# The second norm of a hybrid block: scaled rows and plain transposes in two parts, and a pool whose tiles move by 128 bytes

## The chip, the cores and the metric

The kernel runs on one core of one Trainium2 chip. The metric is the device time of one execution in microseconds, given as the median of several runs. TensorE is called PE (its weight loads PEld), VectorE DVE, ScalarE ACT, GpSimd POOL and SyncE SP; SP's queue issues nearly all transfers of the part that is changed.

## The reference

The block computes one layer on 1024 tokens of width 1024, in float32:

```python
u = modulate(rms_norm(h, ln1_g), shift1, scale1)
mix = token_mixer(u, ...)                  # attention and a recurrent mix, gated, then @ w_o
h = h + gate1[:, None, :] * mix
u2 = modulate(rms_norm(h, ln2_g), shift2, scale2)
h = h + gate2[:, None, :] * conv_ffn(u2, w_up, conv_w, conv_b, w_down)
return rms_norm(h, final_g)

def rms_norm(x, gain):
    return x * rsqrt(mean(x * x, axis=-1) + 1e-6) * gain

def modulate(xn, shift, scale):
    return xn * (1 + scale[:, None, :]) + shift[:, None, :]
```

`conv_ffn` multiplies `u2` (1024x1024) with `w_up` (1024x5632), applies a convolution of width 3 along the tokens, SiLU and a gate, and multiplies with `w_down` (2816x1024). The change concerns the third and fourth line: how `u2` comes out of `h`.

## The kernel before, in words

**Numbers.** A float32 matrix product is made of three products in a faster format (`F32R`): each operand is split into a high and a low part (`split`: ACT casts the high part, DVE subtracts it), and the parts are multiplied high by high, low by high and high by low (`PARTS`). A product of two plain float32 operands (`mm` with F32 tiles) is the other form.

**Stages.** The first norm and the projections, attention and the recurrent mix, the gated branches (`br_part`), then the part that matters here: the output projection with `w_o` (`wo_mm`, `wo_row`), the second norm with its turn (`norm2`, `turn2`), the feed-forward's first product for 22 column tiles of 128 (`up_product`), its second product (`dn_mm`) and the last norm.

**The output projection.** The tokens are eight row tiles of 128, `t` = 0 to 7. For a row tile 48 products of 128x512 (8 `kt`, two column halves `c`, three parts) fill two PSUM banks. The stationary operands are the merged rows, high and low (`mg_hl`; the low part of rows 0 to 3 is `mgl` in pool `se`), the moving ones `wo_hi` and `wo_lo`. Row tiles 0 to 2 are interleaved, and between them stand 16 products of one column with the modulation vectors (`mod_2`, `mod_part_steps`). `wo_row` then takes the row tile: per column half, DVE multiplies PSUM by the gate and adds the result to `h_sb[t]`, and ACT squares it and leaves the row sums in a column of `ssq`. The temporary `x` comes from `row_tmp` for `t` below 5, and from the tag `xq` behind it. SP stores the row to `d_h[t]`, from where the last stage reads it.

**The second norm and the turn.** `norm2(half)` adds the two column halves of the row sums of four row tiles, makes the factors with two ACT instructions (`rms_rstd`) and, on DVE, four diagonal matrices of 128x128 in the tile `dg`: the identity times the factor of each row. `turn2(half, kt, ...)` then makes one bank of `u2` turned: four float32 products of a 128x128 block of `h_sb` (stationary) with that row tile's diagonal matrix (moving), which turns the block and scales its columns by the factors at once. ACT takes the bank out with the modulation's scale and shift (`A2`, `m2`), by row of the turned block. A half needs 8 banks, or 32 products.

**Order.** PE's instructions run in the order written. The first half's turns stand between row tile 4's and row tile 5's products. Each bank is split into the feed-forward's operands `B11` (pool tiles `b`) and `B21` (tiles `f`). Behind that point the order of SP, DVE, ACT and POOL is the written one too; ahead of it a scheduler puts the instructions of those four in order. Behind row tile 7's products, `norm2(1)` runs on DVE and ACT while PE makes the feed-forward's first two products (`X` and `W` of column tile 0); the second half's turns follow in two groups of 16 products, with column tile 1's product `X` between them and `W` behind them.

**The feed-forward's first product** uses Strassen's scheme in Winograd's form: seven products per column tile in place of eight. Its moving operands are sums of the halves of `u2`, each split into high and low: `T3`, `T2`, `T4`, `T1`, `B22`, `B11` and `B21`. DVE and ACT make `T3`, `T2`, `T4`, `T1` and `B22` behind the second half's turns, while PE runs the first products of column tiles 0 and 1 (`T_split`). The low parts of `T1` lie in `e1` and `e5`, the high parts of `B22` in `e2` and `e3`; in the profile they are `T_e` and `B_e`, and the parts of the same operands in the pool `sm` are `T_m` and `B_m`. The stationary operands are sums of pieces of `w_up`, split too (`up_make`), from two loads per column tile (`up_load`); those of tile 1 are loaded into the slots that `h_sb[0]` and `h_sb[1]` had. All 12 products of one of the seven share a bank, and the profile shows them as `X`, `Y` or `W` by its name. DVE's subtractions and ACT's casts for the next stationary operands run a few products ahead (`up_ahead`).

**Pools.** The pool `se` (variable `hp`) holds the tags `e0` to `e5`, `xq` (five buffers), `s` (two), `dg` (one) and the tile `ssq2` of 128 bytes per partition. A tile's place follows from the order in which tags are first used; `ssq2` was the last.

Of the kernel before, what the change touches and what calls it, by code (L numbers as in the profile page):

```python
# [9 lines left out]
F32 = mybir.dt.float32  # L10
F32R = mybir.dt.float32r
AF = mybir.ActivationFunctionType
ALU = mybir.AluOpType
# [4 lines left out]
KT = 8  # L18
NH = 512
# [113 lines left out]
def hybrid_block(ctx: ExitStack, tc: tile.TileContext, a, out):  # L133
    nc = tc.nc
# [3 lines left out]
    def mm(o, lhsT, rhs, start, stop, more=False):  # L138

        weave.mm_cost(o, lhsT, rhs)  # L140
        nc.tensor.matmul(o, lhsT, rhs, start=start, stop=stop, skip_group_check=more)  # L141

    def transpose(o, i, eye):
        weave.now += 0.84 * max(math.prod(i.shape[1:]), i.shape[0])
        nc.tensor.transpose(o, i, eye)
# [4 lines left out]
    tt, stt, ts = nc.vector.tensor_tensor, nc.vector.scalar_tensor_tensor, nc.vector.tensor_scalar  # L150
# [24 lines left out]
    ident, ones = f32(eye_r), f32(C("ones"))  # L175
# [33 lines left out]
    m2 = cp.tile([128, 16], F32, name="m2")  # L209
    A2 = cp.tile([128, 8], F32, name="A2")  # L210
# [135 lines left out]
    with ExitStack() as es:  # L346
# [66 lines left out]
        with tc.tile_pool(name="st", bufs=1) as st, tc.tile_pool(name="stp", bufs=2, space=PS) as stp, \  # L413
                tc.manual_schedule(engines={mybir.EngineType.SP, mybir.EngineType.DVE, mybir.EngineType.Activation}):
            ssq = st.tile([128, 8], F32, name="ssq")
# [765 lines left out]
    def bank(k, name):  # L1181
        return pb.tile([128, NH], F32, tag="big", name=name) if k > 5 else pz.tile([128, NH], F32, tag=f"p{k}", name=name)
# [47 lines left out]
    ww_st.close()  # L1230
    pools["m"] = ctx.enter_context(tc.tile_pool(name="sm", bufs=1, side="right", reuse_waits="tile"))
    pools["e"] = hp = ctx.enter_context(tc.tile_pool(name="se", bufs=1, side="right", reuse_waits="tile"))

    def pairs(tags, name, dt=F32R):

        ts_ = [slot(tag, f"{name}_{tag}", dt) for tag in tags]
        return [ts_[k // 2][:, k % 2 * NH : k % 2 * NH + NH] for k in range(2 * len(tags))]
# [6 lines left out]
    def split(hi, lo, src):  # L1244
        nc.scalar.copy(hi, src)  # L1245
        tt(lo, src, f32(hi), op=ALU.subtract)  # L1246
# [3 lines left out]
    wo = {}  # L1250
# [56 lines left out]
    for x in range(2):  # L1307
        for n in range(8):
            if x or n:
                k = 8 * x + n + 1  # L1310
# [26 lines left out]

    d_h = dr.tile([8, 128, D], F32, name="d_h")
    d_g = dr.tile([7, 128, NP, NH], F32, name="d_g")
    ssq = hp.tile([128, 32], F32, name="ssq2")  # L1340
    def norm2(half):

        dg = hp.tile([128, NH], F32, tag="dg", name=f"dg{half}", bufs=1).rearrange("p (j s) -> p j s", s=128)
        hs = slice(half * 4, half * 4 + 4)
        rs = slice(8 + half * 4, 12 + half * 4)
        tt(ssq[:, rs], ssq[:, rs], ssq[:, hs], op=ALU.add)
        rms_rstd(ssq[:, rs], ssq[:, rs])
        for j in range(4):
            ts(dg[:, j, :], ident, ssq[:, rs][:, j : j + 1], None, op0=ALU.mult)
        return dg  # L1350

    def turn2(half, kt, dg, k, dst):

        ps = bank(k, f"tr{half}_{kt}")
        for j in range(4):
            mm(ps[:, j * 128 : j * 128 + 128], h_sb[half * 4 + j][:, kt * 128 : kt * 128 + 128], dg[:, j, :], start=True, stop=True)
        nc.scalar.activation(dst, ps, AF.Identity, scale=A2[:, kt : kt + 1], bias=m2[:, kt : kt + 1])


    PARTS = ((0, 0), (1, 0), (0, 1))  # L1360
# [13 lines left out]
    def wo_row(t, ps):  # L1374

        for c in range(2):
            cs = slice(c * NH, c * NH + NH)
            x, h = row_tmp[2 * t + c] if t < 5 else hp.tile([128, NH], F32, tag="xq", name=f"wo{t}_{c}", bufs=5), h_sb[t][:, cs]
            tt(x, ps[c], g1b[:, cs], op=ALU.mult)
            tt(h, h, x, op=ALU.add)  # L1380
            nc.scalar.activation(x, h, AF.Square, accum_out=ssq[:, 8 * c + t : 8 * c + t + 1])
        nc.sync.dma_start(d_h[t], h_sb[t])
# [3 lines left out]
    def T_tiles(key, tags):  # L1386
        T[key] = halves(tags, key)
# [243 lines left out]
    for t in range(4, 8):  # L1631
        h_load(t)
    up_load(0)
    dg = norm2(0)
    ps = wo_do(4, 0)
    wo_row(4, ps)

    T_tiles("B11", [f"b{k}" for k in range(4)])
    T_tiles("B21", [f"f{k}" for k in range(4)])
    uf = pairs(("e2", "e3", "e1", "e5"), "uf", F32)  # L1640
    for kt in range(KT):
        turn2(0, kt, dg, 4 + kt % 4, uf[kt])
        split(*(T["B11" if kt < 4 else "B21"][x][kt % 4] for x in range(2)), uf[kt])
    up_load(1)
    ctx.enter_context(tc.manual_schedule(engines={mybir.EngineType.SP, mybir.EngineType.DVE, mybir.EngineType.Activation,
                                                  mybir.EngineType.Pool}))
    for t, k in ((5, 2), (6, 6), (7, 4)):
# [4 lines left out]
            for f in up_ahead(2 * (t - 4)):  # L1652
                f()
        wo_row(t, ps)
    dg = norm2(1)


    early = pairs(("a7",), "Ze", F32)
    steps = up_to(len(plan))
    t1, b21 = uf[0:4], uf[4:]  # L1660
    U = [pairs(tags, f"u2{j}", F32) for j, tags in enumerate((("m8", "m9"), ("m10", "m11")))]
    T_tiles("T3", [f"h{k}" for k in range(4)])

    def T_split(key, srcs, sums=()):
# [10 lines left out]
    for n in range(4):  # L1675
        up_evac(*next(steps))
        if n == 1:
            for f in up_ahead(8):
                f()
        if n in (1, 2):  # L1680
            kts = (0, 1) if n == 1 else (2, 3)
            for kt in kts:
                for j in range(2):
                    turn2(1, kt + 4 * j, dg, 2 + kt % 2 * 2 + j, U[j][kt])
            for kt in kts:
                tt(t1[kt], U[0][kt], t1[kt], op=ALU.subtract)
                tt(U[0][kt], U[1][kt], U[0][kt], op=ALU.subtract)
                nc.scalar.copy(T["T3"][0][kt], U[0][kt])
                if kt % 2:
                    for x in kts:  # L1690
                        tt(T["T3"][1][x], U[0][x], f32(T["T3"][0][x]), op=ALU.subtract)
# [291 lines left out]
```

## Time and profile before

| what | value |
|---|---|
| median of 3 runs | 1682.1 us |
| runs | 1679.19, 1686.33, 1682.1 us |
| profiled execution, first to last instruction (span) | 1679.9 us |
| PE busy | 1630.3 us (97% of the span) |
| DVE busy | 1219.1 us (73%) |
| ACT busy | 806.3 us (48%) |
| granted TensorE clock, mean | 0.993 |
| second norm's turns, first half | 993.57 to 1000.63 us |
| second norm's turns, second half | 1038.90 to 1042.38 and 1045.25 to 1048.73 us |

The page gives the profiled execution no time beside its span. The span lies 2.2 us under the median of the runs and inside their range.

How to read the rows: a time is in microseconds from the span's start. In a timeline a row has start, length, engine, line, operation, out<-in, shape and count; instructions of one kind are merged, and the length runs from the first one's start to the last one's end. In brackets stands how long the engine had been idle before and what ended that. Matmuls are pipelined, so that a single one's length is more than its distance to the next: distances are taken from starts. In the list by line a row ends with the busy time, the mean length in ns and the idle time ahead of it. In the chain a row has start, length, engine, output and line. Line 141 is the helper `mm` and line 145 the helper `transpose`, so PE's rows are told apart by tile names, in which buffer numbers are left out.

### The profile page before, as it was taken

The numbers are of one execution on the slowest core, as the hardware profiler recorded it, in microseconds if no ns is written. First come the engines' busy times: TensorE is split into PE (matmuls) and PEld (weight loads), VectorE is DVE, ScalarE is ACT, GpSimd is POOL, SyncE is SP. The second block draws the span as 40 slices with busy tenths as digits, with TensorE's granted clock in tenths as the row PEclk, the third lists the DMA queues.
The fourth block names the chain that finished last, engine by engine and source line by source line (L and its number), as shares of the span: only waits on it lengthen the run. The fifth ranks groups of instructions, "written<-read, shape, count | busy, mean of one in ns | idle before, by whom it ended". The sixth has DMA issues, their size and how long they took to land.

```text
span 1679.9 us, 26265 instructions
## 1 busy us (share of the span) xinstructions
PE 1630.3 (97%) x9870; PEld 1344.6 (80%) x9870; DVE 1219.1 (73%) x2402; ACT 806.3 (48%) x1481; POOL 131.2 (8%) x151
## 2 busy tenths in 40 slices
PE   7999999999999999999999999999999999999998
PEld 7777777787877778888878888888888888888886
DVE  5786787878866635888778455897777777786677
ACT  5563334434445446676633243654444444455455
POOL 0011001111111011212022000000000000000000
PEclk9999999999999999999999999999999999999999
DMA  8487644443332228434197420133322323584463
GB/s 332 143 322 233 181 124 123 130 120 98 100 112 88 89 67 202 126 108 128 35 335 262 177 88 38 63 120 111 109 95 94 119 95 107 182 276 152 130 211 108
DMA packets 121503, 240.79 MB, mean 143 GB/s; under 512 B 40032, under 2 KB 48608, under 8 KB 121376
## 3 DMA queue, kind: packets, MB, share of 16 engines
q1 hardware_dynamic: 112896, 220.74, 40.2%
q0 software_dynamic: 8480, 18.37, 4.3%
q8 instruction: 78, 1.28, 0.3%
q14 instruction: 49, 0.40, 0.1%
HBM read 173.51 MB, written 65.54 MB: 142 GB/s over the span
## 4 chain that ended last, share of the span: by engine, by line
PE 74%; DVE 14%; DMA 5%; ACT 3%; issue 2%; SPq 1%; DVEq 0%; ACTq 0%
PE X L141 13%; PE D L141 12%; PE Y L141 6%; PE wo L141 5%; PE ps_rkv L141 5%; PE br L141 5%; PE gt L141 4%; PE W L141 3%; PE rk_ps L141 3%; PE qk L141 2%; PE lg L141 2%; PE ov L141 2%; DVE E L780 2%; DVE t L778 2%; PE tr L141 2%
## 5 line engine op out<-in xcount | busy, mean ns | idle before, releaser
L141 PE MATMUL D<-op,op 128*128 128x512 f32 x924 | 209.8, 389 | 0.0
L141 PEld LDWEIGHTS D<-op,op 128*128 128x128 f32 x924 | 173.3, 188 | 36.3 <-DVE op L1246 0.3
L141 PE MATMUL X<-T_m,S 128*128 128x512 f32 x440 | 107.2, 390 | 0.2 <-ACT x L1522 0.2
L141 PEld LDWEIGHTS X<-T_m,S 128*128 128x128 f32 x440 | 82.4, 188 | 18.3 <-ACT x L1522 0.6
L1245 ACT CAST op<-g 128x512 fp32r<-128x512 f32 x77 | 47.8, 621 | 73.7 <-PE D L141 48.5
L1246 DVE TENSOR_TENSOR op<-g,op 128x512 fp32r<-128x512 f32 x77 | 53.0, 688 | 41.4 <-ACT op L1245 41.1
L1482 DVE SCALAR_TENSOR_TENSOR c<-ab,vec,c 128x512 f32<-128x512 f32 x88 | 65.9, 749 | 19.5 <-ACT c L1485 17.9
L778 DVE TENSOR_TENSOR t<-E,M 128x60 f32<-128x60 f32 (+24 forms) x248 | 57.6, 232 | 25.7 <-DMA M<-sm 20.3
L1446 DVE TENSOR_TENSOR S<-ur,S 128x512 fp32r<-128x512 f32 x66 | 45.5, 691 | 35.9 <-ACT S L1442 35.8
L1442 ACT CAST S<-ur 128x512 fp32r<-128x512 f32 x66 | 41.0, 622 | 55.8 <-DVE ur L1435 30.6
L1446 DVE TENSOR_TENSOR A<-ur,A 128x512 fp32r<-128x512 f32 x64 | 44.0, 688 | 30.9 <-ACT A L1442 30.7
L274 DVE TENSOR_TENSOR lo_in<-raw_in,hi_in 128x512 fp32r<-128x512 f32 x84 | 56.5, 712 | 12.5 <-PE gt L141 4.6
L141 PE MATMUL Y<-T_h,A 128*128 128x512 f32 x264 | 63.4, 389 | 0.0
L141 PE MATMUL Y<-T_h,S 128*128 128x512 f32 x264 | 63.3, 389 | 0.0
L272 ACT CAST hi_in<-raw_in 128x1024 fp32r<-128x1024 f32 x42 | 43.8, 1047 | 40.1 <-PE ps_rkv L141 23.2
L1048 ACT ACTIVATE P<-lg,nm 128x896 f32<-128x896 f32 (+3 forms) x64 | 47.5, 743 | 29.0 <-DVE nm L1044 20.8
L141 PE MATMUL X<-B_b,A 128*128 128x512 f32 x252 | 60.8, 390 | 0.0
L141 PE MATMUL W<-B_f,A 128*128 128x512 f32 x252 | 60.6, 389 | 0.0
L780 DVE TENSOR_TENSOR E<-E,t 128x60 f32<-128x60 f32 (+24 forms) x248 | 54.9, 221 | 5.7
L141 PEld LDWEIGHTS Y<-T_h,A 128*128 128x128 f32 x264 | 49.5, 188 | 10.4
L141 PEld LDWEIGHTS Y<-T_h,S 128*128 128x128 f32 x264 | 49.5, 188 | 10.3
L1442 ACT CAST A<-ur 128x512 fp32r<-128x512 f32 x64 | 39.9, 623 | 34.1 <-PE X L141 29.4
(475 smaller groups left out, 4130.9 us busy)
## 6 DMA issues: line engine op xcount, KB each, us to landing
raw_in<-in_w_in SPq DMA_DIRECT2D x50, 512.0 KB, 3.9
wm<-in_w_mod SPq DMA_DIRECT2D x48, 512.0 KB, 7.2
ur<-in_w_up SPq DMA_DIRECT2D x44, 512.0 KB, 4.2
g<-d_g SPq DMA_DIRECT2D x35, 512.0 KB, 4.1
d_g<-gs SPq DMA_DIRECT2D x44, 256.0 KB, 2.0
d_g<-c SPq DMA_DIRECT2D x33, 256.0 KB, 4.4
d_st<-qh SPq DMA_DIRECT2D x64, 128.0 KB, 2.4
stA<-d_st POOLq DMA_DIRECT2D x8, 1024.0 KB, 6.4
```

Of the source, the lines that this page charges most:

```text
L141: nc.tensor.matmul(o, lhsT, rhs, start=start, stop=stop, skip_group_check=more)
L272: nc.scalar.copy(hi, raw)
L274: nc.vector.tensor_tensor(lo[:, c : c + NH], raw[:, c : c + NH], f32(hi[:, c : c + NH]), op=ALU.subtract)
L778: tt(tv, E32[:, 0:J, s : s + 1].to_broadcast([128, J, W]), M32[:, s : s + 1, s + 1 : 32].to_broadcast([128, J, W]), op=ALU.mult)
L780: tt(E32[:, 0:J, s + 1 : 32], E32[:, 0:J, s + 1 : 32], tv, op=ALU.add)
L1048: nc.scalar.activation(e[:, 0:n], lg[:, 0:n], AF.Exp, bias=nm[:, 0:1], accum_out=nm[:, 1:2])
L1245: nc.scalar.copy(hi, src)
L1246: tt(lo, src, f32(hi), op=ALU.subtract)
L1442: nc.scalar.copy(hi, src)
L1446: tt(lo, src, f32(hi), op=ALU.subtract)
L1482: stt(c, ab[:, x + hf * NH : x + hf * NH + NH], V("conv_w", 22 * x + i), c, op0=ALU.mult, op1=ALU.add)
```

## The change

- `norm2(t0, t1)` adds the sums and makes the factors of row tiles `t0` to `t1 - 1`, and no diagonal matrices. It is called for 0 to 3, for 4 to 6 and for 7.
- `scale_row(t)` multiplies a row tile by its factor: tiles 0 to 6 in place, on DVE, over 1024 columns; tile 7 into the slot `m11`, half on DVE and half on ACT.
- `turn2` takes several banks at a time and fills them with transposes against the identity. In the first half ACT and DVE take the banks out in turn (`split_evac`); in the second ACT alone, as before. In the second half's first group row tile 7's blocks come last, behind those of the other three.
- The first half is turned in two parts of four banks: `kt` 0 to 3 where all eight were, and 4 to 7 behind row tile 5's product, into banks 4, 5, 0 and 1.
- For row tiles 5 to 7 `wo_row` takes its first temporary from the tag `dg`, which is free now, and its second from `xq`.
- `ssq2` is the first tile of the pool `se`. The other tiles of that pool start 128 bytes further on than before, and which of the five `xq` buffers a tile gets changes with the row temporaries.

```diff
     pools["e"] = hp = ctx.enter_context(tc.tile_pool(name="se", bufs=1, side="right", reuse_waits="tile"))
+    ssq = hp.tile([128, 32], F32, name="ssq2")
...
-    ssq = hp.tile([128, 32], F32, name="ssq2")
-    def norm2(half):
-
-        dg = hp.tile([128, NH], F32, tag="dg", name=f"dg{half}", bufs=1).rearrange("p (j s) -> p j s", s=128)
-        hs = slice(half * 4, half * 4 + 4)
-        rs = slice(8 + half * 4, 12 + half * 4)
+    def norm2(t0, t1):
+
+        hs, rs = slice(t0, t1), slice(8 + t0, 8 + t1)
         tt(ssq[:, rs], ssq[:, rs], ssq[:, hs], op=ALU.add)
         rms_rstd(ssq[:, rs], ssq[:, rs])
-        for j in range(4):
-            ts(dg[:, j, :], ident, ssq[:, rs][:, j : j + 1], None, op0=ALU.mult)
-        return dg
-
-    def turn2(half, kt, dg, k, dst):
-
-        ps = bank(k, f"tr{half}_{kt}")
-        for j in range(4):
-            mm(ps[:, j * 128 : j * 128 + 128], h_sb[half * 4 + j][:, kt * 128 : kt * 128 + 128], dg[:, j, :], start=True, stop=True)
-        nc.scalar.activation(dst, ps, AF.Identity, scale=A2[:, kt : kt + 1], bias=m2[:, kt : kt + 1])
+
+    normed = {}
+
+    def scale_row(t, dst=None):
+        r = ssq[:, 8 + t : 9 + t]
+        if dst is None:
+            ts(h_sb[t], h_sb[t], r, None, op0=ALU.mult)
+            dst = [h_sb[t][:, c * NH : c * NH + NH] for c in range(2)]
+        else:
+            ts(dst[0], h_sb[t][:, 0:NH], r, None, op0=ALU.mult)
+            nc.scalar.activation(dst[1], h_sb[t][:, NH:], AF.Copy, scale=r)
+        normed[t] = dst
+
+    def turn2(half, kts, ks, dsts, rows=((0, 1, 2, 3),), split_evac=False):
+
+        pss = [bank(k, f"tr{half}_{kt}") for kt, k in zip(kts, ks)]
+        for js in rows:
+            for kt, ps in zip(kts, pss):
+                for j in js:
+                    c0 = kt % 4 * 128
+                    transpose(ps[:, j * 128 : j * 128 + 128], normed[half * 4 + j][kt // 4][:, c0 : c0 + 128], ident)
+        for n, (kt, ps, dst) in enumerate(zip(kts, pss, dsts)):
+            A, B = A2[:, kt : kt + 1], m2[:, kt : kt + 1]
+            if split_evac and n % 2:
+                ts(dst, ps, A, B, op0=ALU.mult, op1=ALU.add)
+            else:
+                nc.scalar.activation(dst, ps, AF.Identity, scale=A, bias=B)
...
-            x, h = row_tmp[2 * t + c] if t < 5 else hp.tile([128, NH], F32, tag="xq", name=f"wo{t}_{c}", bufs=5), h_sb[t][:, cs]
+            x, h = row_tmp[2 * t + c] if t < 5 else hp.tile([128, NH], F32, tag=("dg", "xq")[c], name=f"wo{t}_{c}", bufs=(1, 5)[c]), h_sb[t][:, cs]
...
-    dg = norm2(0)
+    norm2(0, 4)
+    for t in range(4):
+        scale_row(t)
     ps = wo_do(4, 0)
     wo_row(4, ps)
...
-    for kt in range(KT):
-        turn2(0, kt, dg, 4 + kt % 4, uf[kt])
-        split(*(T["B11" if kt < 4 else "B21"][x][kt % 4] for x in range(2)), uf[kt])
+
+    def turn_first(kts, ks):
+        turn2(0, kts, ks, [uf[kt] for kt in kts], split_evac=True)
+        for kt in kts:
+            split(*(T["B11" if kt < 4 else "B21"][x][kt % 4] for x in range(2)), uf[kt])
+
+    turn_first(range(4), (4, 5, 6, 7))
     up_load(1)
...
         wo_row(t, ps)
-    dg = norm2(1)
+        if t == 5:
+            turn_first(range(4, 8), (4, 5, 0, 1))
+        elif t == 6:
+            norm2(4, 7)
+            for r in (4, 5, 6):
+                scale_row(r)
...
     U = [pairs(tags, f"u2{j}", F32) for j, tags in enumerate((("m8", "m9"), ("m10", "m11")))]
+    norm2(7, 8)
+    scale_row(7, U[1][2:])
...
             kts = (0, 1) if n == 1 else (2, 3)
-            for kt in kts:
-                for j in range(2):
-                    turn2(1, kt + 4 * j, dg, 2 + kt % 2 * 2 + j, U[j][kt])
+            turn2(1, [kt + 4 * j for kt in kts for j in range(2)], (2, 3, 4, 5), [U[j][kt] for kt in kts for j in range(2)],
+                  rows=((0, 1, 2), (3,)) if n == 1 else ((0, 1, 2, 3),))
```

## The prediction

> **What bounds the kernel now.** I read the page first, then the busy time by stage around the second norm, then the chain that ended last in the same stretch. A row of the second fence has a stretch and its length in us, the busy us of PE, PEld, DVE, ACT and POOL, then the granted clock, the DMA share and GB/s.
>
> ```profile
> span 1679.9 us, 26265 instructions
> PE 1630.3 (97%) x9870; PEld 1344.6 (80%) x9870; DVE 1219.1 (73%) x2402; ACT 806.3 (48%) x1481; POOL 131.2 (8%) x151
> ```
> ```profile
> 1000.63:1033.37 32.74, 32.74 (x147) 27.12 (x146) 13.59 (x21) 9.82 (x21) 0.00 (x0) 1.00 0.17 65
> 1038.90:1051.60 12.70, 12.70 (x89) 11.66 (x88) 11.47 (x20) 10.30 (x17) 0.00 (x0) 1.00 0.00 1
> 1051.60:1071.06 19.46, 19.44 (x86) 15.68 (x84) 18.08 (x30) 13.12 (x24) 0.00 (x0) 1.00 0.09 28
> 1100.00:1600.00 500.00, 500.00 (x2198) 412.26 (x2197) 377.75 (x604) 237.71 (x409) 0.00 (x0) 1.00 0.40 133
> ```
> ```profile
> 1045.41 3.59 PE tr L141 x32
> 1049.02 0.79 ACT u_m L1357
> ...
> 1083.87 0.71 ACT c L1485
> 1085.11 3.04 PE X L141 x12
> ```
>
> PE carries the kernel: busy in all of 1000.63:1033.37 and 1100:1600. What it saves there comes off the end. The chain adds the exception. Behind the second pair of turns it leaves PE at 1049.02, runs through ACT and DVE alone, and returns at 1085.11. PE looks busy there too (19.44 of 19.46), but DVE is busy for 18.08 of the same 19.46: the two are level, and a shorter PE alone only uncovers DVE and ACT.
>
> **The change, step by step. The first half's turns.** The 32 products with the diagonal tile become 32 transposes, 16 ahead of row tile 5's output product and 16 behind it.
>
> ```profile
> 993.57 7.30 PE L141 MATMUL tr<-dg,h_sb 128*128 128x128 f32 x64
> 1000.63 0.71 PE L141 MATMUL wo<-wo_hi,mg_m 128*128 128x512 f32 x2
> L145 PE MATMUL tp<-cst,P x288: 270/272/330, 656.8 to 837.3; 128*128 128x128 f32 x144
> 707.38 0.82 PE L145 MATMUL tp<-cst,P 128*128 128x128 f32 x6
> ```
>
> A product with `dg` leaves two matmul records (64 for 32), started 7.06/64 = 0.110 us apart. A transpose of the attention, with the same identity and shape, leaves one (the program issues 288). Six end 0.82 us after the first starts and one lasts 0.27, so (0.82 - 0.27)/5 = 0.11 us apart. The 32 cost 3.5 us in place of 7.06: 3.5 us saved on a PE that waits for nothing until 1033. The bounds are 3.3 and 3.7, for what the edges of two groups may add or hide.
>
> What covers the new work in front of them: `norm2(0, 4)` loses four 0.28 us products on DVE and gains four products over whole rows, each of which overwrites its row and so waits for that row's store.
>
> ```profile
> L220 DVE TENSOR_SCALAR acc<-wm,sc 128x1024 f32<-128x1024 f32 x2 | 1.5, 753 | 2.3 <-DMA wm<-in_w_mod 2.3
> L1265 DVE TENSOR_SCALAR acc<-wm,sc 128x1024 f32<-128x1024 f32 x2 | 2.5, 1264 | 0.0
> L1382 SPq DMA_DIRECT2D d_h<-h_sb x1: 319/319/319, 984.8 to 984.8; - x1
> d_h<-h_sb SPq DMA_DIRECT2D x8, 512.0 KB, 2.6
> ur<-in_w_up SPq DMA_DIRECT2D x2, 512.0 KB, 3.4
> 1038.25 0.87 DVE L1349 TENSOR_SCALAR dg<-cst,ssq 128x128 f32<-128x128 f32 x4 [0.60 <-ACT ssq L299]
> ```
>
> Four at 0.75 us (1.26 at worst) from about 986.4, the last not before 984.8 + 2.6 = 987.4, end by 989.5 (991.5 at worst). PE asks for them at 993.57, and only row 4's sums stand behind them on DVE, with their operands ready about 993. So nothing is added; if the cover went, each us of delay would be one on PE. The turn's evacuations are shared between ACT and DVE, and both have 10.9 us of row 5's and row 6's products to do them in. The order on SP's queue stays, and POOL issues nothing here, but the load of `w_up` tile 1 now waits for the second group's transposes, which read the same slots: until 993.57 + 1.76 + 10.88 + 1.76 = 1008.0 (a row's product takes 10.88, below). It lands 3.4 us later. DVE's sums on it stand ahead of row 6's, which PE releases 10.88 us behind 1008, so 7 us cover it; row 5's store, queued behind it on SP, has its data only about then.
>
> **The second half's turns.** The 32 transposes save 6.96 - 3.5 = 3.4 us of PE time; the question is what of it survives DVE and ACT.
>
> ```profile
> 1035.22 0.69 DVE L1379 TENSOR_TENSOR wo<-wo,g1b 128x512 f32<-128x512 f32 x1 [0.84 <-ACT wo L1381]
> 1038.12 0.57 ACT L1522 COPY x<-X 128x512 f32<-128x512 f32 x1
> 1039.24 0.69 DVE L1446 TENSOR_TENSOR S<-s,S 128x512 fp32r<-128x512 f32 x1
> 1041.70 2.78 ACT L1357 ACTIVATE u_m<-tr,m,A 128x512 f32<-128x512 f32 x4
> 1046.77 3.02 ACT L1357 ACTIVATE u_m<-tr,m,A 128x512 f32<-128x512 f32 x4
> L1840 ACT ACTIVATE xtm<-xtm,ssq 128x512 f32<-128x512 f32 x4 | 2.9, 723 | 0.1
> ```
>
> Rows 4 to 6 get their own call of `norm2` and are scaled during row 7's product. DVE then waits for row 6's store, with row 7's sums queued behind: an estimate from row 7's own times is some 3 us to the store, 2.6 to its landing and 2.3 for three rows, 8 of the 10.9 us that row 7's product covers. Only row 7 is left on the path. Its two temporaries now lie in two buffers, so the 0.84 us wait at 1035.22 goes and its factor comes about 0.9 earlier. Then ACT scales half a row (0.72 by the `xtm` row) where it did nothing, which delays the copy of `X` (1038.12) and the casts behind it: of the 0.9 gained some 0.3 is left. DVE's operation at 1039.24 waits for such a cast, and DVE is nearly full from there on (11.47 of 12.70 above), so the first evacuations (1041.70) move up by 0.3 too. The second four start behind DVE again, also 0.3 earlier; they took 3.02 against 2.78 because they waited for PE, and that wait goes: 0.2 more. Behind them DVE and ACT have the work they had. So the chain at 1049.02 moves by about 0.45 us, and so does its return to PE at 1085. PE idles some 3 us of its 3.4 in short waits between 1049 and 1068. I take 0.45. The bounds are -0.4 (ACT's extra 0.72 cancels the gain of 0.9 and delays more than I count) and 3.4 (no chain at all); the chain's rows lie nearer the first.
>
> **The 128 bytes.** `ssq2` is now the first tile of the pool `se` and was its last, so every other tile there moves. In the built program they started on multiples of 256 bytes in a partition, while nearly all other operand tiles of this part start 128 bytes off such a multiple; now these do too. The trace shows two paces for one shape:
>
> ```profile
> 971.60 0.40 PE L141 MATMUL wo<-wo_hi,mgh_f 128*128 128x512 f32 x1
> 982.69 0.61 PE L141 MATMUL wo<-wo_hi,mg_m 128*128 128x512 f32 x2
> 1093.43 1.98 PE L141 MATMUL X<-T_m,S 128*128 128x512 f32 x8
> 1095.24 1.09 PE L141 MATMUL X<-T_e,S 128*128 128x512 f32 x4
> 1096.16 2.90 PE L141 MATMUL X<-B_b,A 128*128 128x512 f32 x12
> 1101.62 2.02 PE L141 MATMUL X<-B_e,S 128*128 128x512 f32 x8
> 1103.48 1.08 PE L141 MATMUL X<-B_m,S 128*128 128x512 f32 x4
> 1104.40 2.88 PE L141 MATMUL X<-T_m,S 128*128 128x512 f32 x12
> 1107.12 1.07 PE L141 MATMUL W<-B_f,A 128*128 128x512 f32 x4
> ```
>
> Row 3's 48 products, a third with weights `mgl` from `se`, take 982.69 - 971.60 = 11.09 us. Row 4's 48 (982.69 to 993.57), none from it, take 10.88. That is 0.21 a row, 0.84 over rows 0 to 3. In the feed-forward the product with `B22` (8 `B_e`, 4 `B_m`) takes 2.78, that with `T1` 2.73, the others 2.72: 0.07 per column tile, 1.4 us over the some 20 behind 1085 (before that PE waits anyway). I take 2.2 us together: every slow group has an operand in the moved pool, and the like groups without one are at 226.7 ns. The bounds are 2.3 and, if place is not the cause or the new place is worse by as much again, -1.5.
>
> [...] The trace shows two paces, but no run here has moved a tile.
>
> **The sum.** 3.5 + 0.45 + 2.2 = 6.2 us, so the span goes from 1679.9 to 1673.7. The page gives no time beside its span, which is 2.2 below the median of the runs, 1682.1 (1679.2 to 1686.3). Off that median it is 1675.9.
>
> **The rivals.** A: the second half pays in full, because DVE and ACT had hidden slack. For it: PE shows no idle time there. Against: the chain's 36 us without PE. The sum gains 2.95 more: 1673.0.
>
> B: the move by 128 bytes does nothing (that part does not do what it might). For it: no row shows one tile in two places. Against: the slow pace appears in the output product and in the feed-forward alike, and only with that pool's tiles. 1682.1 - 4.0 = 1678.1.
>
> C, which ends slower: the clock is halved around the turns.
>
> ```profile
> 473.47:476.88 3.41, 1.25 (x33) 1.21 (x34) 2.63 (x6) 0.64 (x2) 0.00 (x0) 1.00 0.39 86
> 476.88:480.30 3.42, 3.42 (x9) 2.68 (x10) 0.00 (x0) 2.51 (x5) 1.27 (x1) 0.50 0.37 103
> 944.51:947.92 3.41, 3.41 (x28) 3.23 (x27) 0.37 (x2) 0.00 (x0) 0.00 (x0) 1.00 0.73 298
> 947.92:954.75 6.83, 6.83 (x23) 5.77 (x23) 0.33 (x2) 0.00 (x0) 0.00 (x0) 0.50 0.01 5
> ```
>
> Where PE was busy for 1.25 of 3.41 us, the granted clock was 0.50 in the next 3.42. Behind the matmuls of one column in `mod_part_steps` it was 0.50 for 6.83, at a loss of 3.4. The turns are 1.8 us each, between dense products. If transposes counted as little as one-column matmuls and each of the three places (993, 1006, 1039 to 1052) cost such a stretch, 10.2 us would go, less the 3 that PE has spare in the last: 7.2 against 6.2 gained, 1683.1. From the third place on it decides. Against: a 1.8 us group leaves half of any 3.41 us dense, and the uncovered waits come between products.
>
> [...]
>
> **How the numbers follow.** Forecast 0.60, A 0.14, B 0.20, C 0.06. The unknown terms give gains from 3.3 - 0.4 - 1.5 = 1.4 to 3.7 + 3.4 + 2.3 = 9.4, times from 1672.7 to 1680.7. The runs before lie up to 4.2 us from their median, so I give 1670.5 to 1681.5; C's end is left out. Half a per cent, 8.4 us (1673.7 and 1690.5), is about what tells a change here from none. Faster by more: A, and the forecast where the median falls 2 us low: 0.20. Slower by more: C with further such stretches, 0.03. Within: 0.77.
>
> **What would show it.** In the profile after: 16 transpose records per group, 0.11 us apart; no PE wait before the first group; the start of the first feed-forward product 4.3 us earlier (3.5 + 0.84); a PE that waits in short pieces, 3 us together, between the second pair of turns and the first products with `T1`; `B_e` groups at 2.72 us per twelve; a granted clock of 1.00 throughout. Wrong would be: no such waits (A), `B_e` and row 3 at their old pace (B), 0.50 behind a turn (C), or PE waiting at the first group, which would mean that the stores hold the rows.

## The result, and the profile after

The changed kernel takes 1675.0 us (median of 13 runs, 1671.2 to 1679.4) where the kernel before takes 1679.5 us (13 runs, 1676.5 to 1686.3). The ratio is 0.9965, with a 95% interval of 0.9953 to 0.9978: faster by 0.35%, or 5.9 us (3.7 to 7.9; the two medians alone lie 4.5 us apart), inside the half per cent that I had set as the bound. The profiled execution has a span of 1673.2 us.

First the page's head, then TensorE's timeline of the changed kernel.

```profile
span 1673.2 us, 26130 instructions
PE 1626.0 (97%) x9806; PEld 1341.4 (80%) x9806; DVE 1224.8 (73%) x2407; ACT 804.6 (48%) x1480; POOL 130.5 (8%) x151
```
```profile
970.97 0.39 PE L141 MATMUL wo<-wo_hi,mgh_f 128*128 128x512 f32 x1
...
981.85 0.61 PE L141 MATMUL wo<-wo_hi,mg_m 128*128 128x512 f32 x2
...
992.73 1.91 PE L145 MATMUL tr<-cst,h_sb 128*128 128x128 f32 x16
1005.38 1.91 PE L145 MATMUL tr<-cst,h_sb 128*128 128x128 f32 x16
1028.93 2.89 PE L141 MATMUL X<-B_b,A 128*128 128x512 f32 x12
...
1044.20 0.73 PE L141 MATMUL Y<-T_h,S 128*128 128x512 f32 x2 [0.62 <-ACT u_m L1372]
1045.38 0.50 PE L141 MATMUL Y<-T_h,S 128*128 128x512 f32 x1 [0.44 <-ACT T_h L1715]
1046.44 6.69 PE L141 MATMUL Y<-T_h,S 128*128 128x512 f32 x21 [0.56 <-ACT T_h L1715]
1052.97 5.60 PE L141 MATMUL X<-T_m,S 128*128 128x512 f32 x24
...
1069.29 1.98 PE L141 MATMUL X<-B_e,S 128*128 128x512 f32 x8
...
1074.73 2.88 PE L141 MATMUL X<-B_b,A 128*128 128x512 f32 x12
1077.45 2.88 PE L141 MATMUL Y<-T_h,S 128*128 128x512 f32 x12
1080.32 3.01 PE L141 MATMUL X<-T_m,S 128*128 128x512 f32 x12
```

Each group of turns has 16 records where it had 32, 0.11 us apart, and no wait stands ahead of the first. Row tile 3 (970.97 to 981.85) takes 10.88 us where it took 11.09. The waits that were to come behind the second turns are there, three of them, 1.62 us together, ahead of and inside the first products with `T3`. The 21 products behind the third wait take 6.53 us (1046.44 to 1052.97), though 21 products at 0.227 us apart are 4.77. The windows of 3.41 us show what the clock did: busy us of PE, PEld, DVE, ACT and POOL, the granted clock, then the DMA share and GB/s.

```profile
1043.45:1046.86 3.41, 1.79 (x6) 0.86 (x6) 3.12 (x6) 2.50 (x5) 0.00 (x0) 1.00 0.00 0
1046.86:1050.27 3.41, 3.41 (x10) 2.67 (x9) 3.33 (x7) 1.76 (x3) 0.00 (x0) 0.50 0.00 0
```

PE was busy for 1.79 us of the first window, and in the next one the granted clock was 0.50: 1.7 us lost. So PE looks busy there and is slow. Behind the turns the clock held. The window of the first group:

```profile
992.26:995.67 3.41, 3.41 (x25) 3.05 (x24) 3.41 (x6) 2.21 (x4) 0.00 (x0) 1.00 0.00 0
```

Transposes fill 1.67 us of it (992.73 to 994.40), more than the 1.62 us of waits that cost the clock above, and the clock was 1.00 in this window and in the next.

DVE's and ACT's rows of the changed kernel, the short chain behind row tile 7 and the second group's evacuations, answer those at 1037 to 1047 of before. The first fence is the row of before that starts the factor step:

```profile
1037.48 0.17 DVE L1346 TENSOR_TENSOR ssq<-ssq 128x4 f32<-128x4 f32 x1 [0.85 <-ACT wo L1381]
```
```profile
985.56 2.74 DVE L1352 TENSOR_SCALAR h_sb<-h_sb,ssq 128x1024 f32<-128x1024 f32 x4 [0.60 <-ACT ssq L299]
...
1031.99 0.16 DVE L1344 TENSOR_TENSOR ssq<-ssq 128x1 f32<-128x1 f32 x1 [0.79 <-ACT wo L1396]
...
1034.49 0.69 DVE L1461 TENSOR_TENSOR S<-s,S 128x512 fp32r<-128x512 f32 x1 [1.26 <-ACT S L1457]
```
```profile
1032.75 0.73 ACT L1356 ACTIVATE u_m<-h_sb,ssq 128x512 f32<-128x512 f32 x1
1033.38 0.56 ACT L1537 COPY x<-X 128x512 f32<-128x512 f32 x1
...
1042.03 2.79 ACT L1372 ACTIVATE u_m<-tr,m,A 128x512 f32<-128x512 f32 x4
```

But for the pace of row tiles 0 to 2, everything ahead of row tile 3 is the same work in all kernels of this study, but its start lay anywhere from 964.3 to 971.8 us in their profiles. That is more than the whole gain, so I read the gain by stretches between PE's own starts, where a difference of 0.05 us repeats:

| stretch | before | after | gain |
|---|---|---|---|
| row tile 3's 48 products | 11.09 | 10.88 | 0.21, and four rows have it: 0.84 |
| a: row tile 4's first product to column tile 0's `X` | 50.68 | 47.09 | 3.59 |
| b: from there to column tile 2's second `X` product (1085.11; 1080.32) | 51.74 | 51.38 | 0.36 |
| c: from there to the second stage's first product (1462.49; 1455.81) | 377.38 | 375.49 | 1.89 |
| d: from there to the end | 217.37 | 217.41 | -0.04 |

The sum is 6.6 us, inside the interval's 3.7 to 7.9. Of the four row tiles in the first line only row tile 3 is timed by itself; the first 48 products of the three ahead of it, all at a clock of 1.00, go from 11.09 us (931.57 to 942.66) to 10.88 (933.09 to 943.97) too. `move_384`, `phase_64`, `all_zero`, `cut` and `fill_turns` were run once each, so for these there are stretches and no ratio. Below, "a + b" is the stretch from row tile 4 to column tile 2's second `X` product: 102.42 before, 98.47 after. Its two ends are the products `wo<-wo_hi,mg_m` and `X<-T_m,S` of the rows shown. Stretch c ends with these two, of before and of after:

```profile
1462.49 0.39 PE L141 MATMUL D<-op,op 128*128 128x512 f32 x1
```
```profile
1455.81 0.39 PE L141 MATMUL D<-op,op 128*128 128x512 f32 x1
```

### The profile page after: what moved, and what is told of

Its sections match the earlier page's. It is cut to its first block, busy times and chain, and to the rows that moved or that the text cites. A ratio compares the mean times of both kernels' runs of the same rounds, so it can differ in the third digit from the quotient of the medians.

```text
span 1673.2 us, 26130 instructions
## 1 busy us (share of the span) xinstructions
PE 1626.0 (97%) x9806; PEld 1341.4 (80%) x9806; DVE 1224.8 (73%) x2407; ACT 804.6 (48%) x1480; POOL 130.5 (8%) x151
## 3 DMA queue, kind: packets, MB, share of 16 engines
q8 instruction: 77, 1.26, 0.3%
## 4 chain that ended last, share of the span: by engine, by line
PE 74%; DVE 14%; DMA 6%; ACT 3%; issue 2%; SPq 2%; DVEq 0%; ACTq 0%
PE X L141 14%; PE D L141 13%; PE Y L141 7%; PE wo L141 5%; PE ps_rkv L141 5%; PE br L141 5%; PE gt L141 4%; PE rk_ps L141 3%; PE W L141 3%; PE qk L141 2%; PE lg L141 2%; PE ov L141 2%; PE tp L145 2%; DVE E L780 1%; DVE t L778 1%
## 5 line engine op out<-in xcount | busy, mean ns | idle before, releaser
L272 ACT CAST hi_in<-raw_in 128x1024 fp32r<-128x1024 f32 x42 | 43.8, 1047 | 42.5 <-PE ps_rkv L141 25.0
```

Source lines behind the costliest of these rows:

```text
L272: nc.scalar.copy(hi, raw)
```

## Experiments on the 128 bytes

Two questions were open: whether the move does anything by itself, and what it is about the place that counts.

**The move alone.** The kernel before, with one line moved:

```diff
     pools["e"] = hp = ctx.enter_context(tc.tile_pool(name="se", bufs=1, side="right", reuse_waits="tile"))
+    ssq = hp.tile([128, 32], F32, name="ssq2")
...
-    ssq = hp.tile([128, 32], F32, name="ssq2")
```

> The kernel before, with only ssq2 allocated first in the pool se. Theory (the start of an operand within 256 bytes sets the pace): row tile 3's 48 output products take 10.88 us (11.09 before), the second half's chain stays (102.3 to 102.4 us from row tile 4's first product to the product X of column tile 2; 102.42 before, 98.47 in the changed kernel), and from there to the first product of the feed-forward's second stage 375.5 us (377.38 before, 375.49 in the changed kernel). Together 2.7 us less than before, ratio 0.9984. Rival (the place does nothing; the changed kernel's faster feed-forward comes from the other assignment of the xq buffers or from elsewhere): 11.09, 102.4 and 377.4, ratio 1.000.

```profile
967.62 0.39 PE L141 MATMUL wo<-wo_hi,mgh_f 128*128 128x512 f32 x1
...
978.50 0.39 PE L141 MATMUL wo<-wo_hi,mg_m 128*128 128x512 f32 x1
...
1080.89 0.50 PE L141 MATMUL X<-T_m,S 128*128 128x512 f32 x1 [0.33 <-ACT x L1522]
...
1456.41 0.39 PE L141 MATMUL D<-op,op 128*128 128x512 f32 x1
```

Row tile 3 takes 10.88 us, c is 375.5 and a + b is 102.39 us. Ratio 0.9981 (0.9968 to 0.9994). The move alone gives 0.84 + 1.87 us and nothing in a + b, where the chain of DVE and ACT hides it: PE waits 0.33 us for ACT ahead of column tile 2's `X` in place of 0.16.

**Another 128 bytes.** A tile of 128 bytes more behind `ssq2`:

```diff
     ssq = hp.tile([128, 32], F32, name="ssq2")
+    hp.tile([128, 32], F32, name="pad_e")
```

> The changed kernel with 128 more bytes behind ssq2, so that the other tiles of the pool lie 256 bytes further on than before and start on multiples of 256 again. Theory (what counts is the start modulo 256): the slow pace is back, row tile 3 at 11.09 us, the stretch behind column tile 2's X at 377.4 us, 2.7 us lost against the changed kernel: some 1677.7 us where the changed kernel had 1675.0. Rival (any move away from the old place helps): 10.88 and 375.5 as in the changed kernel.

Row tile 3 took 10.88 us, c 375.49, ratio 0.9965 (0.9951 to 0.9979). But the edit did not do what I meant: a pool on this side is placed from its upper end, so what is added in front only lowers `ssq2`, and all operands lie where the changed kernel has them. The run repeats that kernel and says that the place of `ssq2` itself does not matter. To move the operands, bytes go to the pool's end.

**Three other places.** `pad_e` is allocated last in `se`: 384 bytes put its tiles on multiples of 256 bytes at a new place, 64 bytes put them 64 behind such a multiple. The first diff is that of 384 bytes; with 64 it has 16 in place of 96. For the third kernel (second diff, without `pad_e`), 128 bytes more go ahead of the pools on the left and to the upper end of those on the right, so that the operands of the output product and of the feed-forward's first product, in every pool, start on multiples of 256 (all but the weights of column tile 0's `W`, of which more below).

```diff
+    hp.tile([128, 96], F32, name="pad_e")
     def norm2(t0, t1):
```
```diff
-    ctx.enter_context(tc.tile_pool(name="top", bufs=1, side="right")).tile([128, 24], F32, name="top")
+    ctx.enter_context(tc.tile_pool(name="top", bufs=1, side="right")).tile([128, 56], F32, name="top")
...
+    ctx.enter_context(tc.tile_pool(name="padp", bufs=1)).tile([128, 32], F32, name="pad_l")
     fxp = ctx.enter_context(tc.tile_pool(name="fxp", bufs=1, reuse_waits="tile"))
```

> The changed kernel with 384 more bytes at the upper end of the pool se, from which the pool is placed: its tiles lie 384 bytes lower than in the changed kernel (256 lower than before) and start on multiples of 256 bytes again, at a place that neither kernel had. Theory (the start modulo 256 counts): row tile 3 at 11.09 us, the stretch from column tile 2's X to the second stage at 377.4 us. Rival (only the old place was slow): 10.88 and 375.5.

> The changed kernel with 64 bytes at the upper end of se: its tiles start 64 bytes behind a multiple of 256, the other operands 128 behind one. Theory (only a start on a multiple of 256 is slow): 10.88 and 375.5 us. Rival (every start that differs from the other operand's is slow): 11.0 to 11.1 and 376.4 to 377.4.

> The changed kernel with 128 bytes more ahead of the pools on the left and at the upper end of those on the right, so that the operands of the output product and of the feed-forward's first products all start on multiples of 256 bytes, those of se too. Theory (a start on a multiple of 256 is slow in itself): row tile 3 at 11.1 to 11.3 us, row tile 4 as slow, and some 384 us from column tile 2's X to the second stage (1656 products by 5 ns more). Rival (slow is what differs from the other operand): 10.88 and 375.5, as with all operands 128 off.

The same four starts, with `phase_64` first and `all_zero` second:

```profile
969.15 0.40 PE L141 MATMUL wo<-wo_hi,mgh_f 128*128 128x512 f32 x1
...
980.24 0.40 PE L141 MATMUL wo<-wo_hi,mg_m 128*128 128x512 f32 x1
...
1078.82 0.44 PE L141 MATMUL X<-T_m,S 128*128 128x512 f32 x1
...
1456.64 0.39 PE L141 MATMUL D<-op,op 128*128 128x512 f32 x1
```
```profile
966.90 0.39 PE L141 MATMUL wo<-wo_hi,mgh_f 128*128 128x512 f32 x1
...
977.78 0.39 PE L141 MATMUL wo<-wo_hi,mg_m 128*128 128x512 f32 x1
...
1076.22 0.50 PE L141 MATMUL X<-T_m,S 128*128 128x512 f32 x1
...
1451.72 0.39 PE L141 MATMUL D<-op,op 128*128 128x512 f32 x1
```

| kernel | tiles of `se`, from a multiple of 256 | other operands | row tile 3 | c |
|---|---|---|---|---|
| before | 0 | 128 | 11.09 | 377.38 |
| changed | 128 | 128 | 10.88 | 375.49 |
| move_384 | 0 | 128 | 11.09 | 377.36 |
| phase_64 | 64 | 128 | 11.09 | 377.82 |
| all_zero | 0 | 0 | 10.88 | 375.50 |

My theory, that a start on a multiple of 256 is slow in itself, held for `move_384` and fell with the other two. With all operands on such multiples the pace is the fast one, and 64 bytes behind one is as slow as 0, or a little slower than I gave the rival (377.82 against 377.4 at most). The rival stands: **in these kernels, slow was what differed, modulo 256 bytes, from the operand that it met.** The medians of the distance between starts, in the output product and the feed-forward's first product of before and after, say the same: 227 ns where both operands start 128 bytes behind a multiple of 256, 229 to 235 where one is at 0 and the other at 128, in either role (in the kernel before 232 with `B_e` as moving operand and 234 with `mgl` as stationary one). With both at 0, the 48 products of row tile 3 are 227 ns apart on average (`all_zero`, 10.88 us); with `mgl` at 64 and the rest at 128 it is 231 (`phase_64`, 11.09 us). A distance of 256 cost nothing where it was measured: in the changed kernel as built, `B_e` at 126592 and its weights from 60288 on lie 256 apart modulo 512, and keep 227. One group differs in the changed kernel too: the weights of column tile 0's `W` start on a multiple of 256 there and its moving tiles 128 behind one, and its products are 232 ns apart, as before. What on the chip this comes from, the runs do not show. Products beside a slow one lose a little as well: in the kernel before, the first with `mgh_f`, ahead of one with `mgl`, was at 233, and `B_m`, behind `B_e`, at 231; both are at 226 to 227 in the changed kernel.

## Experiments on the second half's turns

The question is what the 3.5 us that PE saves in the second half became.

**The second half undone.** The changed kernel with the second half's own part taken back:

```diff
-        elif t == 6:
-            norm2(4, 7)
-            for r in (4, 5, 6):
-                scale_row(r)
...
-    norm2(7, 8)
-    scale_row(7, U[1][2:])
+    norm2(4, 8)
+    dg = hp.tile([128, NH], F32, tag="dg", name="dg1", bufs=1).rearrange("p (j s) -> p j s", s=128)
+    for j in range(4):
+        ts(dg[:, j, :], ident, ssq[:, 12 + j : 13 + j], None, op0=ALU.mult)
...
-            turn2(1, [kt + 4 * j for kt in kts for j in range(2)], (2, 3, 4, 5), [U[j][kt] for kt in kts for j in range(2)],
-                  rows=((0, 1, 2), (3,)) if n == 1 else ((0, 1, 2, 3),))
+            for kt in kts:
+                for j in range(2):
+                    turn_dg(kt + 4 * j, 2 + kt % 2 * 2 + j, U[j][kt])
```

`turn_dg` is the old `turn2`.

> The changed kernel with the second half as before: one factor step for row tiles 4 to 7 behind row tile 7, four diagonal matrices, products with them in place of transposes. The two buffers for the row temporaries, the first half and the 128 bytes stay. Theory (the chain of DVE and ACT sets this stretch): 98.5 to 98.9 us from row tile 4's first product to column tile 2's X, against 98.47 with the transposes, though TensorE has 3.5 us more to do; no wait of TensorE behind the second turns and a clock of 1.00. Rival (TensorE's time counts here): 101.5 to 102 us.

a + b is 98.80 us and PE goes from the second turns into the products with `T3` without a wait; ratio 0.9968 (0.9956 to 0.9981). Of the 3.5 us of PE time, 0.33 arrives. The two buffers alone bring the factor step 0.92 us earlier here (3.18 us behind column tile 0's `X`, 1027.67 to 1030.85, where it was 4.11 before), but b is 51.72 us against 51.74: ACT's second evacuations wait for the longer turns and take 3.46 us (from 1040.62), where the changed kernel's take 2.79.

**The lost clock, and the chain.** Two edits and both together. `fill` puts 12 products behind column tile 1's `W`, into a bank that nobody reads; `cut` takes eight subtractions from DVE: it leaves out the low parts of `T2` and `T4`, and the products read the high parts in their place, so a part of its sums is wrong.

```diff
+        if (i, k) == (1, 2):
+            pf = bank(2, "fill")
+            for n in range(12):
+                mm(pf, A[0][:, n % 4 * 128 : n % 4 * 128 + 128], B[0][n % 4], start=n == 0, stop=n == 11)
```
```diff
         hi, lo = T[key]
+        short = key in ("T2", "T4")
+        if short:
+            T[key] = hi, hi
...
-            if kt:
+            if kt and not short:
                 tt(lo[kt - 1], srcs[kt - 1], f32(hi[kt - 1]), op=ALU.subtract)
```

> The changed kernel with 12 products more behind column tile 1's W, whose result (bank 2) nobody reads: they stand where TensorE waits in short pieces ahead of and inside the first products with T3, and where the granted clock fell to 0.50 for 3.41 us. Theory (the second half ends with the chain of DVE and ACT, and the lost clock lies in its shadow): the clock stays 1.00, the first 24 products Y take 5.4 us in place of 8.8, but TensorE then waits for ACT ahead of column tile 2's X, some 1.2 us in place of 0.15, and from row tile 4's first product to that product it is 98.4 to 98.6 us as in the changed kernel (98.47). Rival (the lost clock costs time): that stretch shrinks by 1.1 us to 97.4.

> cut_fill without its 12 products: the changed kernel with the low parts of T2 and T4 not made (the products take the high parts in their place, so a part of the sums is wrong). Theory (the lost clock and the chain end level): with the chain shortened alone, TensorE's own way with 3.41 us at a clock of 0.50 sets column tile 2's X, 98.2 to 98.4 us behind row tile 4's first product. Rival (the shorter chain pays by itself): 97.1 us as in cut_fill.

> The 12 products of fill, and DVE relieved: the low parts of T2 and T4 are not made (eight subtractions of 0.61 us; the products take the high parts in their place, so a part of the sums is wrong). Theory (TensorE with its lost clock and the chain of DVE and ACT end level at column tile 2's X, so only both at once show): 97.2 to 97.4 us from row tile 4's first product to column tile 2's X, against 98.46 with the 12 products alone. Rival (something else, a load or a bank, sets that point): 98.4.

| a + b, us | chain as it is | eight subtractions less |
|---|---|---|
| waits and lost clock as they are | 98.47 | 98.41 |
| 12 products in the wait | 98.46 | 97.07 |

Each edit alone moves nothing (0.01 and 0.06 us), both move 1.40. In these executions TensorE with its 1.7 us of lost clock, and the chain of DVE and ACT, reach column tile 2 at the same time. With both it is 97.07, a little under the 97.2 to 97.4 that I expected. PE's rows, of `fill`, then of `cut`, then of `cut_fill`:

```profile
1042.64 2.88 PE L141 MATMUL fill<-B_f,A_1h 128*128 128x512 f32 x12
1045.36 5.60 PE L141 MATMUL Y<-T_h,S 128*128 128x512 f32 x24
1050.81 5.60 PE L141 MATMUL X<-T_m,S 128*128 128x512 f32 x24
1056.24 3.09 PE L141 MATMUL Y<-T_h,A 128*128 128x512 f32 x12
1059.17 2.81 PE L141 MATMUL X<-T_m,S 128*128 128x512 f32 x8
1061.82 1.07 PE L141 MATMUL X<-T_e,S 128*128 128x512 f32 x4
...
1079.52 0.73 PE L141 MATMUL X<-T_m,S 128*128 128x512 f32 x2 [0.31 <-ACT x L1541]
```
```profile
1044.80 6.64 PE L141 MATMUL Y<-T_h,S 128*128 128x512 f32 x21 [0.56 <-ACT T_h L1718]
```
```profile
1045.99 5.60 PE L141 MATMUL Y<-T_h,S 128*128 128x512 f32 x24
```

With the 12 products the clock stays at 1.00 and the 24 products `Y` take 5.45 us. What is gained is handed back in small pieces: the 8 `T_m` products take 2.65 us to the next start where 1.81 would do, the 12 `Y` ahead of them 2.93 where 2.72 would, and the wait ahead of column tile 2's second `X` product is 0.31 us. I had expected all 1.2 us at that one place. `cut` keeps the slow 21 products.

`move_256`, with all operands where the changed kernel has them, is a test of the same without any edit to the work. Its three waits are as long (0.62, 0.44 and 0.56 us), but fall into two windows:

```profile
1038.68:1042.09 3.41, 2.35 (x10) 1.34 (x8) 2.73 (x5) 3.25 (x6) 0.00 (x0) 1.00 0.00 0
1042.09:1045.50 3.41, 2.86 (x12) 2.14 (x13) 3.23 (x6) 1.77 (x3) 0.00 (x0) 1.00 0.00 0
```

With 1.06 us idle in one and 0.55 in the next the clock stayed at 1.00. The 21 products take 4.88 us (1043.04 to 1047.92) in place of 6.53, and a + b is 98.47 us all the same. So the lost clock cost the changed kernel nothing, and with the same waits it was lost in one execution and kept in another, whose windows split them. `cut` had its 1.62 us in one window (1041.59 to 1045.00); with the clock kept it might gain by itself, which no run shows. In `all_zero` 1.38 us in one window were followed by 0.50:

```profile
1039.73:1043.14 3.41, 2.03 (x6) 1.16 (x7) 3.22 (x6) 2.12 (x4) 0.00 (x0) 1.00 0.00 0
1043.14:1046.56 3.42, 3.42 (x10) 2.65 (x9) 3.33 (x6) 1.84 (x3) 0.00 (x0) 0.50 0.00 0
```

Idle time in a window does not settle it alone. Ahead of the part that is changed, the changed kernel has a window with 1.62 us idle too, among products of 128x512 as here, and the clock stayed at 1.00 behind it; so it did in the kernel before with 1.91 us idle, the longest behind which it was kept once PE had started. Each window and the next, of after, then of before:

```profile
865.95:869.36 3.41, 1.79 (x8) 1.54 (x9) 2.63 (x4) 0.00 (x0) 0.85 (x1) 1.00 1.03 416
869.36:872.77 3.41, 3.41 (x17) 2.83 (x16) 3.41 (x5) 0.06 (x1) 0.00 (x0) 1.00 0.98 369
```
```profile
220.88:224.30 3.42, 1.51 (x7) 0.91 (x5) 1.99 (x4) 0.00 (x0) 0.76 (x2) 1.00 0.66 161
224.30:227.71 3.41, 2.51 (x12) 1.83 (x12) 3.06 (x10) 1.00 (x2) 0.19 (x1) 1.00 0.63 210
```

**Do transposes hold the clock?** `fill` with 24 transposes in place of the 12 products:

```diff
-            for n in range(12):
-                mm(pf, A[0][:, n % 4 * 128 : n % 4 * 128 + 128], B[0][n % 4], start=n == 0, stop=n == 11)
+            for n in range(24):
+                transpose(pf[:, n % 4 * 128 : n % 4 * 128 + 128], normed[4 + n % 3][n // 4 % 2][:, n % 4 * 128 : n % 4 * 128 + 128], ident)
```

> fill with 24 transposes of 128x128 in place of the 12 products, 2.6 us of TensorE too. If a transpose counts for the clock as a product does, the clock stays 1.00 as in fill and the first 24 products Y take 5.4 us. If it does not, the 2.6 us count as a wait, the clock falls to 0.50 for 3.41 us and they take 7.1 us. The end of the stretch is 98.4 to 98.5 us either way, since the chain sets it.

The clock changed at 952.4 us in this run, and its windows are 3.413 us long (28 of them lie between two falls of the changed kernel's clock, at 951.28 and 1046.85 us), so one runs from 1044.55 to 1047.96. It and the next, and PE's rows:

```profile
1044.55:1047.96 3.41, 3.41 (x28) 3.24 (x27) 3.22 (x6) 2.22 (x4) 0.00 (x0) 1.00 0.00 0
1047.96:1051.37 3.41, 3.41 (x16) 2.83 (x16) 3.32 (x6) 1.85 (x3) 0.00 (x0) 1.00 0.00 0
```
```profile
1044.25 2.78 PE L145 MATMUL fill<-cst,h_sb 128*128 128x128 f32 x24
1046.79 5.70 PE L141 MATMUL Y<-T_h,S 128*128 128x512 f32 x24
```

2.24 us of that window (1044.55 to 1046.79) are transposes. Where the changed kernel waited for 1.62 us of one, the clock fell; here it stays 1.00, and the `Y` products take 5.54 us. a + b is 98.47 us, as expected either way. No window of before or after with more than 1.91 us idle kept the clock, once PE had started. So in this run these transposes counted as work for the clock.

## A version with a shorter chain

The chain has room ahead of the second turns. In the changed kernel ACT scales half a row (1032.75) and copies `X` (1033.38) before the casts that DVE waits 1.26 us for (1034.49), and copies the second `X` ahead of the second evacuations. `sooner` moves these: DVE scales both halves, and both copies come behind the casts for `T3`. `sooner_swap` also lets PE run column tile 2's `W` before its second `X` product (second diff).

```diff
-            ts(dst[0], h_sb[t][:, 0:NH], r, None, op0=ALU.mult)
-            nc.scalar.activation(dst[1], h_sb[t][:, NH:], AF.Copy, scale=r)
+            for c in range(2):
+                ts(dst[c], h_sb[t][:, c * NH : c * NH + NH], r, None, op0=ALU.mult)
...
+    held = []
     for n in range(4):
-        up_evac(*next(steps))
+        step = next(steps)
+        if step[1] == 1:
+            held.append(step)
+        else:
+            up_evac(*step)
...
+    for step in held:
+        up_evac(*step)
     T_tiles("T2", [f"m{k}" for k in range(4)])
```
```diff
-    plan += [(0, 4), (0, 5), (1, 5), (1, 4), (0, 3), (1, 3)] + [(2, k) for k in (1, 7, 6, 2, 4, 5)]
+    plan += [(0, 4), (0, 5), (1, 5), (1, 4), (0, 3), (1, 3)] + [(2, k) for k in (1, 7, 2, 6, 4, 5)]
```

> The changed kernel with less on ACT ahead of the second turns: DVE scales both halves of row tile 7, and the copies of X of column tiles 0 and 1 move from ahead of the casts and of the second evacuations to behind the casts of T3. Theory (the chain sets the stretch): DVE's first subtraction for S3 comes 0.8 us earlier and the second evacuations another 0.5, and all of it arrives: 97.2 us from row tile 4's first product to column tile 2's X (98.47), 472.7 us from row tile 4 to the second stage (473.96), ratio to the kernel before 0.9958. Rival (TensorE or a later order on ACT sets the end): 98.3 and 473.8.

> sooner, and column tile 2's product W ahead of the product that adds S2 with T2 to its X, so that TensorE has a product more to run while ACT copies X. Theory: the wait ahead of column tile 2's second X product goes, and what TensorE and the chain differ by there comes off too: 471.3 to 472.5 us from row tile 4's first product to the second stage, ratio to the kernel before 0.9950. Rival (the chain returns to TensorE at the next product as late): 472.7.

PE's rows of `sooner`, and the window with its wait:

```profile
1038.92 5.05 PE L141 MATMUL Y<-T_h,S 128*128 128x512 f32 x21 [0.57 <-ACT T_h L1720]
...
1072.79 2.56 PE L141 MATMUL X<-T_m,S 128*128 128x512 f32 x10 [0.31 <-ACT x L1537]
```
```profile
1037.64:1041.06 3.42, 2.85 (x12) 1.99 (x11) 3.25 (x6) 2.59 (x6) 0.00 (x0) 1.00 0.00 0
```

a + b is 97.03 us, 1.44 less than 98.47: a little more than the 1.27 forecast, and all of it arrived. PE still waits ahead of the products with `T3`, but 0.57 us only, and no clock is lost. From row tile 4 to the second stage `sooner` takes 472.52 us and `sooner_swap` 471.91, against 473.96 in the changed kernel and 479.80 before: the swap gives 0.6 us more. Ratios to the kernel before are 0.9961 (0.9947 to 0.9974) and 0.9953 (0.9938 to 0.9969). These intervals overlap that of the changed kernel, so that the two are faster than it by their stretches, and not shown to be by their run times.

## Why the prediction was right, step by step

The forecast was 6.2 us; the stretches sum to 6.6, the ratio gives 5.9. The span was to be 1673.7 and was 1673.2; the median 1675.9 and was 1675.0. The last two agree in part by luck. The 1675.9 was counted from a median of three runs, 1682.1; over thirteen it is 1679.5. And the start of row tile 3, which moves by 7.5 us from profile to profile, lay only 0.63 us apart in these two (971.60 and 970.97). It is the stretches that bear the steps out.

- **The first half, 3.5 us: 3.59.** The turns are at half their records and at the distance of the attention's transposes, and all of it arrives at column tile 0's `X`. The four scalings end at 988.3 and PE asks at 992.73, so 4.4 us of cover were left, about as forecast.
- **The second half, 0.45 us: 0.36**, and `second_undone` shows 0.33 for its own part. The steps of the sum came out one by one, measured against the shift of 4.44 us at column tile 0's `X`: the factor step 1.05 earlier (1037.48 to 1031.99; 0.9 forecast), ACT's copy of `X` 0.30 earlier (1038.12 to 1033.38; 0.3 forecast), the second evacuations 2.79 us long in place of 3.02. The two last did not quite add: DVE's chain ends 0.35 earlier (1049.83 to 1045.04), not 0.45. Nor do the steps stand by themselves: with the two buffers alone the factor step came 0.92 earlier and 0.02 of it arrived, as long as the evacuations waited for PE.
- **Where PE's other 3 us went: the place was right, the form was half wrong.** I forecast 3 us of short waits between 1049 and 1068 and a clock of 1.00 throughout. There were 1.62 us of waits, all ahead of or in the first products with `T3`, and they cost 1.7 us more by the clock, in this execution; in that of `move_256` the same waits cost none. That is rival C's halved clock, behind waits and not behind transposes. It changed no time, because the chain was the limit anyway; with the chain shortened by eight subtractions, the 12 products that keep the clock up are worth 1.34 us (98.41 against 97.07). Behind the turns themselves the clock stayed at 1.00. I had looked for C there, and not at the waits that my own forecast put behind them.
- **The 128 bytes, 2.2 us: 0.84 + 1.89 = 2.73.** Row tile 3 came out to the hundredth. The feed-forward was mis-sized: 0.07 us per column tile by the forecast, 1.89/20 = 0.094 measured. I took all products but those with `B22` and `T1` at 2.72, though the row of the 12 `X<-B_b,A` at 1096.16, which stand behind `T_e`, goes on to 1098.90: 2.74. The changed kernel has 2.72 for them (1074.73 to 1077.45), and that makes the missing 0.02.
- **Rival B** (the move does nothing; its 4.0 us are the 3.5 and 0.45 without the 2.2) is refuted by `move_alone`: the move by 128 bytes takes c from 377.38 to 375.5 us, and one by 64 bytes takes the changed kernel's 375.49 to 377.82 (`phase_64`).
- **Rival A** (the second half pays in full) is refuted by `second_undone`.

## What to carry to other kernels

Before costing a faster operation, find out which engine the next hand-over waits for: two limits that are level show nothing when one of them is moved, and only an edit of both at once shows it. Waits that are forecast on TensorE should be priced with the clock that they may cost, not only with their length, and one profile shows that price for its own execution only: here 1.7 us in one, none in another. And where products of one shape run at two paces, compare the starts of their two operands modulo 256 bytes: a tile of 128 bytes in the right order was worth 2.7 us here.

## What the runs showed of the hardware that I had not expected

- 128x512 products in `F32R` were 227 ns apart where both operands start 128 bytes behind a multiple of 256, and 229 to 235 where one starts on a multiple and the other 128 behind (medians of the output product and the feed-forward's first product, before and after). Over the 48 products of row tile 3 the average was 227 with all on multiples (`all_zero`) and 231 with `mgl` 64 bytes from the others (`phase_64`). Between the places measured, the absolute start made no difference: row tile 3 took 11.09 us in before and `move_384`, 10.88 in after and `all_zero`.
- In the changed kernel 1.62 us of waits in one window of 3.41 us were followed by 3.41 us at a granted clock of 0.50, and so were 1.38 (`all_zero`); 1.06 (`move_256`) and 0.57 (`sooner`) in one window were not, nor were 1.62 in an earlier window of the same profile and 1.91 in one of the kernel before. What else than the idle time of the window decides, these runs do not show.
- With 24 plain float32 transposes in the place of the waits, 2.24 us of them in one window, the clock stayed at 1.00 (`fill_turns`), as it did with 12 products (`fill`).
